# Side streams interleaved at smaller steps, and the decay's 64-row matmuls split over the two halves of the array

## The chip, the cores and the metric

One Trainium2 chip, one core of it. The metric is the time of one execution on the device in microseconds (us), as the median of several runs. TensorE is PE in the profile, VectorE DVE, ScalarE ACT, GpSimd POOL, and SyncE (SP) issues the DMAs.

## The reference

Two layers of a trunk with four gated branches run over 640 tokens: 128 context tokens and 512 latent tokens, of width 1024, in fp32. What a layer computes, cut to what matters here:

```python
h = rmsnorm(x, g_norm) * (1 + scale) + shift
(a_u, a_v, b_r, b_k, b_v, b_wd, b_ad, c_q, c_k, c_v, d_p, z, mg) = split_in(h @ w_in)
# RWKV-7 mixer, for both directions d
decay = exp(-exp(-softplus(-(w0[d] + tanh(b_wd) @ w_up[d])) - 0.5))
a = sigmoid(a0[d] + b_ad @ a_up[d])          # b_ad has ICL_RANK = 64 columns
k_d = k * (1 + (a - 1) * k_a)
S = S * w - (S kk) (kk * a)^T + v k_d^T       # scan over the tokens, o = S r
y_b = group_norm(o_sum) * ln_g + ln_b + bonus
# attention (windowed, with sinks), chunk mixer, pool mixer; then
ys = stack(y_a, y_b, y_c, y_d) * silu(z)
x = x + gate * ((sum over branches of sigmoid(mg) * (ys @ w_up)) @ w_o)
```

## The kernel before

Features lie on the 128 partitions and tokens on the free axis, in two halves `hs[0]` and `hs[1]` of HF = 320 tokens. The large products (`accum`, the **main stream**) take each operand as a high and a low part in fp32r (`hi`, `lo`, and for weights `whi`, `wlo`), three one-pass matmuls of 128x320 for a tile of 128 inputs: 7008 in all, in four `m` banks of PSUM. Weights come as `raw` pieces by DMA; `split` (L435) casts them to `whi` on ACT and subtracts for `wlo` on DVE.

All else is **side streams**: generators that `Clock.run` (L227) advances between steps of the main stream. The order of the whole program is set there, while it is built. `Clock` keeps estimates of when each operand is ready; a side stream that yields is resumed when its estimated time has come, and what stands between two of its yields is issued in one piece. Streams that matter here:

- `normed` (L620): the norm and modulation of x for the next layer, with `rstd_thin` (L599), which sums squares over the partitions by 128x2 matmuls (`x<-cst,nacc` for the sum `acc`, `x<-cst,t` for its last part `more`), takes the root (ACT) and the reciprocal `rst` (DVE), and spreads it over the partitions by transposing matmuls (`x<-cst,rst`, the function `spread`).
- `scan(ft, ...)` (L695), one for each half ft of the mixer's features, one after the other. Its `decay(d)` (L707) is called for both directions: two 64-row matmuls (`x<-adt,pb`, 64x320, fp32) give the learning rate a for the two halves of tokens, each read by three ACT instructions; then the decay `w` by `x<-pb,wdt`, by `x<-cst,A` and by ACT's Exp. Between the directions `vn` is reversed by matmuls with `anti` (`x<-vn,cst`). Then come the masked products (`x<-qr,kb`), 31 dependent steps on DVE that invert the blocks, eight rounds of the recurrence, and at the end `group_norm` (L983) is spawned as a stream of its own (`x<-yb,cst`, then the variance `x<-t,cst`).
- `attention` (L1164): its scores are pairs of 64-row matmuls (`x<-xm`), one head on the lower and one on the upper array rows, each into its own bank.

The side streams share two `x` banks (`X()`), the recurrence and the attention's values the banks `c` and `o`. `head` (L1315) makes `ck`, `cv`, `q0` and `q1`; in layer 0 the first three are accumulated together over all eight tiles of h as these become ready, and `put` then copies them out of PSUM, on ACT and DVE in turn. `adt` holds the mixer's b_ad on partitions 64 to 127, `aup` its weights on the same rows:

```python
px = X()
mm(px[:, 0:HF], ap[64:128, d, ft * P:(ft + 1) * P], adt[64:128, hs[b]])
A.activation(th[:, hs[b]], px[:, 0:HF], AF.Tanh, bias=a0h[:, 2 * d + ft:2 * d + ft + 1], scale=0.5)
```

Of the kernel before, what the change touches and what calls it, by code (L numbers as in the profile page):

```python
# [14 lines left out]
P = 128  # L15
# [44 lines left out]


DRAM = set()


def _box(ap):
# [230 lines left out]
def hybrid_layers_kernel(ctx: ExitStack, tc: tile.TileContext, xt, cond, condb, wm, wt, wa, wb, wo, pa, pb, pc, gfin, kctx, vctx,  # L296
# [302 lines left out]
    def rstd_thin(acc, more=None):  # L599

        ms = X()
        parts = [acc] if more is None else [acc, more]
        for i, o in enumerate((0, P, HF - P)):
            for x in parts:
                mm(ms[:, 2 * i:2 * i + 2], x[:, o:o + P], K("mean")[:, 0:2], start=i == 0 and x is acc,
                   stop=i == 2 and x is parts[-1])
        st = S([P, 6], "rst", 2)
        A.activation(st, ms[:, 0:6], AF.Sqrt, bias=eps[:, 0:1])
        V.reciprocal(st, st)

        def spread():
            bc = X()
            for i, (o, c) in enumerate(((0, 0), (P, 0), (2 * P, C))):
                mm(bc[:, o:min(o + P, HF)], st[:, 2 * i:2 * i + 1].to_broadcast([P, P]), K("ident")[:, c:P])
            A.copy(acc, bc[:, 0:HF])
            return bc

        return spread

    def normed(xs, accs, l, out, bs, ahead, more=None):  # L620
        rs = {}
        for b in bs:
            rs[b] = accs[b]
            if l:
                rstd_thin(accs[b], more)()
        for b in bs:
            out[b] = (S([P, KT, HF], f"hi{b}", dt=F32R), S([P, KT, HF], f"lo{b}", dt=F32R))
            ck.mark(f"hh{l}{b}")
# [42 lines left out]
    def layer(l, h, prb):  # L671
# [23 lines left out]
        def scan(ft, ta, kt, rt, vt):  # L695
# [9 lines left out]
            wup = prm("wup").rearrange("p (f d c) -> p f d c", f=2, d=2)  # L705

            def decay(d):  # L707
                for b in range(2):
                    px = X()
                    mm(px[:, 0:HF], ap[64:128, d, ft * P:(ft + 1) * P], adt[64:128, hs[b]])  # L710
                    A.activation(th[:, hs[b]], px[:, 0:HF], AF.Tanh, bias=a0h[:, 2 * d + ft:2 * d + ft + 1], scale=0.5)
                    A.activation(kd[:, hs[b]], th[:, hs[b]], AF.Identity, bias=kab[:, ft:ft + 1],
                                 scale=kah[:, ft:ft + 1])
                    A.activation(th[:, hs[b]], th[:, hs[b]], AF.Identity, bias=eps[:, 3:4], scale=0.5)
# [70 lines left out]
            for d in range(2):  # L785
# [15 lines left out]
                yield from keys(d)  # L801
                if d == 0:
                    yield from decay(1)
            yield
            for b in range(2):
                px = X()
# [95 lines left out]
            for j in range(8):  # L902
# [78 lines left out]
                state.update(nxt_state)  # L981
                yield
            def group_norm():  # L983
                oc = [X(), X()]
                cen = S([P, 2, HF], "v")
                sqs = []
# [328 lines left out]
        def head():  # L1315
# [17 lines left out]
            if l == 0:  # L1333
# [5 lines left out]
                for k in range(KT):  # L1339
                    turn = k % 4 == 3  # L1340
                    for b, i in [(b, i) for i in range(3) for b in range(2)] if turn else [
                            (b, i) for b in range(2) for i in range(3)]:
                        yield f"h{l}{b}.{k}"
                        yield from accum([out[i][b]], ws[i], k % 4, 1, [rhs_h[b]], k, k == 0, k == KT - 1)
                        if turn and b:
                            if k + 1 < KT:
                                ws[i] = piece(0)
                            else:
                                split(nxt[2] + i)
                yield f"n{l}0"  # L1350
                for i in range(3):
                    for b in range(2):
                        put(HEAD[i], b, out[i][b])
                o = yield from main()
                for b in range(2):
                    put(HEAD[3], b, o[b])
# [47 lines left out]
        o = yield from main()  # L1404
        for b in range(2):
            A.activation(wdt[0:64, hs[b]], o[b][0:64, :], AF.Tanh)
            V.tensor_copy(adt[64:128, hs[b]], o[b][64:128, :])
        ck.mark(f"{L}wa")
        for n, t in (("k0", ta[:, 0]), ("v0", vt), ("r0", ta[:, 2]), ("k1", kx[:, 0]), ("r1", kx[:, 1]), ("v1", kx[:, 2])):
            yield from main_to(t)  # L1410
# [189 lines left out]
def _layout(inputs):  # L1600
# [42 lines left out]
    wup[:, 0:64] = g["rw_w_up"].reshape(NL, 2, 64, 2, P).transpose(0, 2, 3, 1, 4).reshape(NL, 64, 512)  # L1643
    wup[:, 64] = g["rw_w0"].reshape(NL, 2, 2, P).transpose(0, 2, 1, 3).reshape(NL, 512)
    aup = np.zeros((NL, P, 512), np.float32)
    aup[:, 64:] = g["rw_a_up"].transpose(0, 2, 1, 3).reshape(NL, 64, 512)
    pw = np.zeros((NL, P, 2, P), np.float32)
    for gr in range(4):
        r = slice(64 * (gr % 2), 64 * (gr % 2) + 64)
# [38 lines left out]
```

## Time and profile before

| | us |
|---|---|
| median of 3 runs (lowest, highest) | 1394.77 (1393.83, 1397.92) |
| profiled execution, its own time | 1396.28 |
| span from its first to its last instruction | 1394.2 |
| PE busy in the span | 1349.6 (97%), 11350 instructions |
| DVE busy | 925.8 (66%), 2056 instructions |
| ACT busy | 565.3 (41%), 1258 instructions |
| POOL busy | 48.0 (3%), 43 instructions |
| mean granted clock of PE | 0.992 |

Busy times are unions of an engine's instructions. Matmuls overlap, so a matmul's own duration (0.31 us for a main one) is longer than the step to the next (0.147 us). An fp32 matmul shows as two instructions, a transpose or an fp32r matmul as one. The column of idle time counts from the modelled end of the last instruction. A granted clock of 1.00 is 2.4 GHz, of 0.50 it is 1.2 GHz.

### The profile page before, as it was taken

What the parts mean: (1) busy time and instruction counts of PE and PEld (TensorE: products, weight loads), DVE (VectorE), ACT (ScalarE), POOL (GpSimd) and SP (SyncE); (2) the same over time, 40 slices, a digit from 0 to 9 for tenths busy, and PEclk for the clock granted to TensorE, in tenths of its full rate; (3) what the DMA queues carried; (4) which work ended last, traced back from release to release, by engine and by line L of the source; (5) the groups of instructions that cost most, each with busy time, mean ns of one, the idle gap of its engine ahead of it and who ended that gap; (6) DMA issues with size and microseconds to landing.
All of it is one profiled execution on the core that took longest, in us unless ns stands there. A gap on an engine that the chain in (4) does not pass through costs nothing. (4 is left out here: it accounts for less than half of the span.)

```text
span 1394.2 us, 27698 instructions
## 1 busy us (share of the span) xinstructions
PE 1349.6 (97%) x11350; PEld 1259.7 (90%) x11350; DVE 925.8 (66%) x2056; ACT 565.3 (41%) x1258; POOL 48.0 (3%) x43
## 2 busy tenths in 40 slices
PE   5899999999999999999999999999999999999997
PEld 4889889988999988999999988898799998899997
DVE  5766677856777856658876667694377684464474
ACT  5455622234522333325555555223354233332364
POOL 0100010000000000000001001000000000000000
PEclk9999999999999999999999999999999999999998
DMA  9411133421224331751113212433022323144012
GB/s 376 148 54 61 39 108 106 108 81 66 67 88 115 106 94 63 267 187 61 61 62 120 72 54 66 109 87 88 24 60 65 89 83 82 37 157 156 22 39 76
DMA packets 86503, 132.61 MB, mean 95 GB/s; under 512 B 44744, under 2 KB 46152, under 8 KB 84456
## 3 DMA queue, kind: packets, MB, share of 16 engines
q1 hardware_dynamic: 86376, 130.84, 29.9%
q8 instruction: 89, 1.46, 0.4%
q14 instruction: 38, 0.31, 0.1%
HBM read 120.46 MB, written 10.35 MB: 94 GB/s over the span
## 5 line engine op out<-in xcount | busy, mean ns | idle before, releaser
L331 PE MATMUL m<-hi,whi 128*128 128x320 f32 x2064 | 666.1, 323 | 3.3 <-ACT whi L290 1.6
L331 PE MATMUL m<-hi,wlo 128*128 128x320 f32 x2064 | 641.4, 311 | 1.9 <-DVE wlo L290 1.9
L331 PE MATMUL m<-lo,whi 128*128 128x320 f32 x2064 | 640.6, 310 | 2.0 <-DVE lo L290 1.3
L331 PEld LDWEIGHTS m<-hi,whi 128*128 128x128 f32 x2064 | 389.9, 189 | 25.3 <-issue 10.2
L331 PEld LDWEIGHTS m<-lo,whi 128*128 128x128 f32 x2064 | 390.1, 189 | 5.1 <-DVE lo L290 2.0
L331 PEld LDWEIGHTS m<-hi,wlo 128*128 128x128 f32 x2064 | 389.5, 189 | 4.5 <-DVE wlo L290 4.2
L290 ACT CAST whi<-raw 128x640 fp32r<-128x640 f32 (+1 forms) x220 | 148.9, 682 | 282.3 <-PE m L331 262.6
L290 DVE TENSOR_TENSOR wlo<-raw,whi 128x640 fp32r<-128x640 f32 (+1 forms) x220 | 168.1, 769 | 107.6 <-ACT whi L290 104.8
L290 ACT ACTIVATE t<-m 128x320 f32<-128x320 f32 x152 | 64.2, 434 | 87.3 <-PE m L331 87.1
L290 DVE TENSOR_TENSOR kb<-kb 80x31 f32<-80x31 f32 (+15 forms) x248 | 86.2, 348 | 10.2 <-DMA kb<-ad 3.5
L290 DVE SCALAR_TENSOR_TENSOR t<-t,m 128x320 f32<-128x320 f32 x120 | 57.7, 481 | 47.0 <-PE m L331 38.0
L331 PE MATMUL m<-ysh,whi 128*128 128x320 f32 x256 | 82.6, 323 | 0.7 <-DVE t L290 0.7
L290 DVE CUSTOM_DVE_ANT_0 junk<-wt,sil 128x1024 bf16<-128x1024 f32 x64 | 79.2, 1237 | 3.8 <-DMA wt<-wt 3.6
L331 PE MATMUL m<-ysh,wlo 128*128 128x320 f32 x256 | 79.1, 309 | 0.0
L331 PE MATMUL m<-ysl,whi 128*128 128x320 f32 x256 | 79.0, 309 | 0.0
L290 DVE TENSOR_TENSOR xm<-xm,t 128x320 f32<-128x320 f32 x96 | 50.8, 530 | 3.3
L331 PEld LDWEIGHTS m<-ysh,whi 128*128 128x128 f32 x256 | 48.1, 188 | 3.4 <-DVE t L290 0.9
L331 PEld LDWEIGHTS m<-ysl,whi 128*128 128x128 f32 x256 | 48.2, 188 | 0.2
L331 PEld LDWEIGHTS m<-ysh,wlo 128*128 128x128 f32 x256 | 48.1, 188 | 0.0
L290 DVE RECIPROCAL t<-t 128x320 f32<-128x320 f32 x16 | 34.4, 2149 | 19.1 <-ACT t L290 19.1
L290 ACT ACTIVATE vn<-c 64x128 f32<-64x128 f32 x40 | 10.8, 271 | 79.0 <-DVE vn L290 79.0
L290 DVE TENSOR_TENSOR A<-x,cst 128x512 f32<-128x512 f32 x40 | 25.7, 684 | 20.6 <-PE x L331 20.6
(242 smaller groups left out, 1517.8 us busy)
## 6 DMA issues: line engine op xcount, KB each, us to landing
raw<-wb SPq DMA_DIRECT2D x128, 320.0 KB, 2.9
raw<-wa SPq DMA_DIRECT2D x92, 256.0 KB, 2.9
wt<-wt SPq DMA_DIRECT2D x32, 512.0 KB, 4.0
A<-wm SPq DMA_DIRECT2D x4, 1024.0 KB, 9.1
A<-wo SPq DMA_DIRECT2D x8, 512.0 KB, 6.0
xm<-xt SPq DMA_DIRECT2D x4, 640.0 KB
ad<-A SPq DMA_DIRECT2D x8, 320.0 KB
qr<-wm SPq DMA_DIRECT2D x2, 1024.0 KB
```

The lines of the kernel that those rows point to most:

```text
L290: return f(out, *a, **k)
L331: PE.matmul(out, lhsT, rhs, start=start, stop=stop)
```

## The change

The sums in `rstd_thin` go over `acc` first and then over `more`; `normed` yields between the sums and the spread; `decay` issues its two matmuls together, the first half of tokens on array rows 64 to 127 and the second on rows 0 to 63, for which `adt`'s second half and a second copy of `aup` lie on the lower partitions; `scan` yields once more behind the second direction's decay; `group_norm` yields before its first matmul; and `head` in layer 0 puts each tile as soon as its last product is issued.

```diff
+ROWS = (slice(64, 128), slice(0, 64))
...
         parts = [acc] if more is None else [acc, more]
-        for i, o in enumerate((0, P, HF - P)):
-            for x in parts:
+        for x in parts:
+            for i, o in enumerate((0, P, HF - P)):
                 mm(ms[:, 2 * i:2 * i + 2], x[:, o:o + P], K("mean")[:, 0:2], start=i == 0 and x is acc,
                    stop=i == 2 and x is parts[-1])
...
             if l:
-                rstd_thin(accs[b], more)()
+                spread = rstd_thin(accs[b], more)
+                yield
+                spread()
...
             def decay(d):
-                for b in range(2):
-                    px = X()
-                    mm(px[:, 0:HF], ap[64:128, d, ft * P:(ft + 1) * P], adt[64:128, hs[b]])
+                pxs = [X(), X()]
+                for b, px in enumerate(pxs):
+                    mm(px[:, 0:HF], ap[ROWS[b], d, ft * P:(ft + 1) * P], adt[ROWS[b], hs[b]])
+                for b, px in enumerate(pxs):
                     A.activation(th[:, hs[b]], px[:, 0:HF], AF.Tanh, bias=a0h[:, 2 * d + ft:2 * d + ft + 1], scale=0.5)
...
                 yield from keys(d)
                 if d == 0:
                     yield from decay(1)
+                    yield
...
             def group_norm():
+                yield
                 oc = [X(), X()]
...
                         yield from accum([out[i][b]], ws[i], k % 4, 1, [rhs_h[b]], k, k == 0, k == KT - 1)
+                        if k == KT - 1:
+                            yield f"n{l}0"
+                            put(HEAD[i], b, out[i][b])
...
-                yield f"n{l}0"
-                for i in range(3):
-                    for b in range(2):
-                        put(HEAD[i], b, out[i][b])
...
-            V.tensor_copy(adt[64:128, hs[b]], o[b][64:128, :])
+            V.tensor_copy(adt[ROWS[b], hs[b]], o[b][64:128, :])
...
-    aup[:, 64:] = g["rw_a_up"].transpose(0, 2, 1, 3).reshape(NL, 64, 512)
+    for r in ROWS:
+        aup[:, r] = g["rw_a_up"].transpose(0, 2, 1, 3).reshape(NL, 64, 512)
```

As the order comes from the estimates in `Clock`, nearly every piece of the side streams stands beside other main matmuls than before. The main matmuls keep their order; POOL's instructions keep theirs. Of the changes between a matmul of the main stream and one of a side stream there were 520 on PE and are 542; of changes of the array's size (tiles of 128, 64 or 32 rows or columns) between neighbours there were 416 and are 415.

PE in layer 1, at the end of the first scan: the decay of the second scan (`adt,pb`) and the group norm of the first (`yb,cst`). Before:

```order
L331 MATMUL m<-hi_7953,wlo 128x320
L331 MATMUL x<-adt,pb 128x320 x2
L331 MATMUL x<-yb,cst 128x320 x2
L331 MATMUL m<-hi_7571,whi 128x320
L331 MATMUL m<-lo_7572,whi 128x320
```

and now:

```order
L332 MATMUL m<-hi_7971,wlo 128x320
L332 MATMUL x<-adt,pb 128x320 x2
L332 MATMUL m<-hi_7580,whi 128x320
L332 MATMUL m<-lo_7581,whi 128x320
L332 MATMUL m<-hi_7580,wlo 128x320
```

The decay is followed by main matmuls, and `yb,cst` comes after 15 of them. Between `cst,A` and the reversal `vn,cst` no main matmul stood in any of the four scans; now 36, 12, 15 and 12 do.

PE in layer 1, the norm of the second half of tokens (`nacc` and `t` are summed, `rst` is spread). Before:

```order
L331 MATMUL m<-hi_7571,wlo 128x320
L331 MATMUL x<-cst,nacc 128x2
L331 MATMUL x<-cst,t 128x2
L331 MATMUL x<-cst,nacc 128x2
L331 MATMUL x<-cst,t 128x2
L331 MATMUL x<-cst,nacc 128x2
L331 MATMUL x<-cst,t 128x2
L331 MATMUL x<-cst,rst 128x128 x2
L331 MATMUL x<-cst,rst 128x64
L331 MATMUL m<-hi_7571,whi 128x320
```

and now:

```order
L332 MATMUL x<-cst,nacc 128x2 x3
L332 MATMUL x<-cst,t 128x2 x3
L332 MATMUL m<-hi_7580,whi 128x320
L332 MATMUL m<-lo_7581,whi 128x320
L332 MATMUL m<-hi_7580,wlo 128x320
L332 MATMUL m<-hi_7580,whi 128x320
L332 MATMUL m<-lo_7581,whi 128x320
L332 MATMUL m<-hi_7580,wlo 128x320
L332 MATMUL x<-cst,rst 128x128 x2
L332 MATMUL x<-cst,rst 128x64
```

Six main matmuls stand between the sums and the spread.

ACT in layer 0's head (`xm<-m` and `xm<-c` are the copies of ck and q0, `bon<-m` that of cv, `whi` the next weights, `wt<-sil` belongs to the modulation). Before:

```order
L290 ACTIVATE wt<-sil 128x1024
L290 CAST whi<-raw 128x512
L290 ACTIVATE wt<-sil 128x1024
L290 CAST whi<-raw 128x512 x2
L290 COPY xm_642<-m 128x320
L290 COPY bon<-m 128x320
L290 COPY xm_642<-c 128x320
```

and now:

```order
L291 ACTIVATE wt<-sil 128x1024
L291 COPY xm_606<-m 128x320
L291 CAST whi<-raw 128x512
L291 ACTIVATE wt<-sil 128x1024
L291 COPY bon<-m 128x320
L291 CAST whi<-raw 128x512
L291 COPY xm_606<-c 128x320
L291 CAST whi<-raw 128x512 x2
```

The copies stand between the casts. DVE, which makes the second copy of each tile, has them in the same way; there ck's copy and the rotation of ck that follows now come ahead of the low part of q1's second weights.

## Rows read from the trace of the kernel before

**Rows 1.** The page's first part: busy us, share of the span, instructions.
```profile
PE 1349.6 (97%) x11350; PEld 1259.7 (90%) x11350; DVE 925.8 (66%) x2056; ACT 565.3 (41%) x1258; POOL 48.0 (3%) x43
```
**Rows 2.** Waits of PE: who waited for whom, us in total, times, longest.
```profile
PE x L331 <- ACT A L290: 4.9, 6, 1.4
PE x L331 <- DVE rst L290: 2.5, 4, 0.7
```
**Rows 3.** Timeline of PE: start, us until the end, instruction, count; a decay.
```profile
375.98 1.34 PE L331 MATMUL x<-adt,pb 64*128 64x320 f32 x4
...
376.62 0.70 PE L331 MATMUL x<-adt,pb 64*128 64x320 f32 x2
...
376.89 0.43 PE L331 MATMUL x<-adt,pb 64*128 64x320 f32 x1
377.25 0.41 PE L331 MATMUL m<-hi,whi 128*128 128x320 f32 x1
```
**Rows 4.** Timeline of PE: a pair of the attention's scores.
```profile
149.12 0.70 PE L331 MATMUL x<-xm 64*128 64x256 f32 x4
149.75 0.41 PE L331 MATMUL m<-hi,whi 128*128 128x320 f32 x1
```
**Rows 5.** Timeline of PE, layer 0: the reversals of both scans [idle before, releaser].
```profile
168.84 1.41 PE L331 MATMUL x<-vn,cst 64*64 64x512 f32 x8 [1.39 <-ACT A L290]
170.18 0.44 PE L335 MATMUL o<-cst,kbt 128*128 128x128 f32 x2
...
385.15 1.08 PE L331 MATMUL x<-vn,cst 64*64 64x512 f32 x4
...
386.76 0.41 PE L331 MATMUL m<-hi,whi 128*128 128x320 f32 x1
```
**Rows 6.** Timeline of PE, layer 0: the first group norm.
```profile
331.62 0.81 PE L331 MATMUL x<-yb,cst 128*128 128x320 f32 x2
333.31 0.81 PE L331 MATMUL x<-yb,cst 128*128 128x320 f32 x2 [0.89 <-ACT A L290]
...
335.71 1.24 PE L331 MATMUL x<-t,cst 128*128 128x320 f32 x4
```
**Rows 7.** Timeline of PE, layer 1: the first group norm.
```profile
1006.35 1.32 PE L331 MATMUL x<-yb,cst 128*128 128x320 f32 x2 [0.89 <-ACT A L290]
...
1010.33 1.24 PE L331 MATMUL x<-t,cst 128*128 128x320 f32 x4
```
**Rows 8.** Stretches: length, busy of PE, PEld, DVE, ACT, POOL, clock, DMA.
```profile
1006.50:1009.90 3.40, 3.40 (x12) 3.01 (x13) 0.49 (x1) 3.02 (x5) 0.00 (x0) 0.50 0.00 0
...
712.90:716.30 3.40, 3.40 (x16) 3.40 (x15) 1.61 (x3) 1.50 (x4) 0.00 (x0) 0.51 0.78 267
```
**Rows 9.** Timeline of PE: the spread of the second half's norm, layer 1.
```profile
711.56 0.85 PE L331 MATMUL x<-cst,rst 128*128 128x128 f32 x6 [0.68 <-DVE rst L290]
```
**Rows 10.** Timeline of DVE: first and last of the eight rounds behind it.
```profile
715.16 1.00 DVE L290 SCALAR_TENSOR_TENSOR t<-xm,gsc,nacc 128x320 f32<-128x320 f32 x2
...
731.87 0.55 DVE L290 SCALAR_TENSOR_TENSOR lo<-t,shift,hi 128x320 fp32r<-128x320 f32 x1 [0.17 <-ACT hi L290]
```
**Rows 11.** Timeline of PE: layer 0's head, from q0's last matmuls on.
```profile
57.52 0.31 PE L331 MATMUL o<-hi,whi 128*128 128x320 f32 x1
...
57.81 0.31 PE L331 MATMUL o<-hi,wlo 128*128 128x320 f32 x1
59.57 0.41 PE L331 MATMUL m<-hi,whi 128*128 128x320 f32 x1 [1.44 <-ACT xm L290]
...
62.51 0.39 PE L331 MATMUL m<-hi,whi 128*128 128x320 f32 x1
```
**Rows 12.** Timeline of DVE: a product of the modulation, layer 0's head.
```profile
58.92 1.23 DVE L290 TENSOR_TENSOR sil<-wt,sil 128x1024 f32<-128x1024 f32 x1
```
**Rows 13.** Timeline of PE and of DVE, layer 1: the second group norm.
```profile
1213.28 1.24 PE L331 MATMUL x<-yb,cst 128*128 128x320 f32 x4
...
1224.06 0.55 DVE L290 SCALAR_TENSOR_TENSOR yb<-v,pb,bon 128x320 f32<-128x320 f32 x1
```

## The prediction

> **What bounds the kernel now.** I read the page first: the share of each engine says that TensorE (PE) is busy for 1349.6 of 1394.2 us [rows 1]. So a DMA, a cast or a vector operation is worth nothing here unless PE waits for it, and there are only two ways to gain: make PE's own work shorter, or take away places where it stands still. The second view is therefore the list of waits of PE alone; two lines of it belong to places that the change touches: matmuls into the x banks wait 4.9 us in all for ACT to read the bank, and 2.5 us for the reciprocal `rst` [rows 2]. The third is the timeline of PE at each place that the diff names, because the idle column understates a wait: a matmul's modelled end lies well behind its successor's start, so I count from start to start. The step of a main matmul (128x320, one pass) is 0.147 us there: 57.52 to 57.81 is two steps [rows 11]. The fourth is the order of the program before and after: it shows where each piece of the side streams now stands between the 7008 main matmuls, which themselves keep their order.
>
> **1. The decay's two matmuls on different array rows.** Eight calls, each with two 64-row matmuls of 320 columns, four instructions in the trace. On the same rows they run one after the other: from 375.98 to the next main matmul at 377.25, 1.27 us [rows 3]; the third and the fourth stand 0.27 apart, which is what one of them streams. The trace has the new form in the attention's scores, where the two heads stand on the lower and the upper rows and write two banks: four instructions of 256 columns need only 0.63 us from 149.12 to the next main matmul at 149.75 [rows 4]. One instruction of 256 columns streams 4/5 as long as one of 320, so four in line would be about 1.27 - 4 x 0.05 = 1.06 us: the pair saves two of four steps. For 320 columns that is 1.27 - 2 x 0.27 = 0.73, a gain of 0.54 a call and **-4.3 us** for eight. It lies on PE's own path, so nothing has to hide anything. The bounds are two steps (-4.3) and one (-2.2); I take two, as the scores have the same form to the letter.
>
> Here a rule of the Trainium skill speaks for less. TensorE: Matmul & The Clock Gate, Part 3, says that matmuls start and end strictly in the order of issue. If the two instructions of one matmul were issued ahead of the two of the other, only the middle ones could overlap, and this term would be -2.2. The scores' row disagrees: with one overlap their block would be about 1.06 - 0.21 = 0.85, not 0.63.
>
> **2. A yield behind the second decay.** The reversal of v (`anti`) took the x bank that the decay's Exp still read. In both layers' first scan PE is idle 1.39 us for ACT [rows 5]; once begun, the block takes 1.34 there, from 168.84 to 170.18. In the second scans it takes 1.61, from 385.15 to 386.76, so 0.27 more, for the same bank. In the new order at least 12 main matmuls (1.76 us) stand between `cst,A` and the reversal at all four places, more than the wait was. 2 x 1.39 + 2 x 0.27 = **-3.3**; what covers it is main work that PE has to do anyway.
>
> **3. A yield ahead of the group norm.** Its first matmuls followed the decay of the second scan with nothing between. The first norm matmul starts at 331.62 and the second at 333.31, 1.69 later [rows 6], where two instructions of 320 columns need 0.54. The difference is 1.15; as a block of its own the norm costs one more change of array size, about 0.1 (the decay's last instruction is followed after 0.36 instead of 0.27 [rows 3]). I take -1.05 in each layer, **-2.1**, bounds -0.9, the idle time shown, and -1.15. Fifteen main matmuls (2.2 us) now stand in the gap. In layer 1 the same stall has a second price. From the second norm matmul to the variance matmul there are 12 main matmuls in both layers: 2.40 us in layer 0 [rows 6], 3.98 in layer 1 [rows 7]. In that stretch the granted clock is 0.50, the level of 1.2 GHz [rows 8], and PE had just stood still. Without the stall I expect no such stretch: **-1.6**, bounds 0 and -1.6.
>
> **4. The norm of layer 1: all of acc first, and a yield ahead of the spread.** The 12 tiny matmuls cost the same in either order. The wait for the reciprocal is idle time of 0.68 in the second half's norm, at 711.56 [rows 9], and the first half's norm has one of the same kind; six main matmuls (0.88 us) now fill each. After the second one the clock also falls to 0.51 for 3.4 us [rows 8], which costs about 13 steps x 0.12 = 1.56. But what is late next here is the chain of DVE and ACT that makes h of the second half: eight rounds from 715.16 to the last lo at 731.87 [rows 10], about 2.1 us each, while PE gets through its 96 covered matmuls in 14 us and must then wait for h. In the new order the spread falls directly behind the last matmul of ck and should be through near 712.8; with ACT's copy of it and a multiplication that now stands first on DVE the chain starts near 713.9, some 1.2 earlier, an estimate. So of 0.7 + 1.56 only 1.2 comes through; for the first half, whose chain is as tight, I take 0.5. Together **-1.7**, bounds -0.5 and -3.9.
>
> **5. Earlier puts in layer 0's head.** q1's first matmul waits for a bank of ck: 57.81 to 59.57 instead of 0.147, thus 1.6, and the transposes of cv then wait about 1.0 more until 62.51 [rows 11]. With the copies behind each tile both go. But the copies and ck's rotation now stand in DVE's queue ahead of the low part of q1's second weights, with the second multiplication of sil before them (1.23 at 58.92 [rows 12], then a shuffle and two products). Adding these up, cv's second copy ends near 62.5 and the low part near 63.1, where PE would want the copy at 61.7. PE is through main matmul 168 and the transposes at about 63.3, where before it was at 64.8 (62.51 and 15 more main steps): **-1.5**, bounds 0 and -2.6. Of the DMAs, ck's output now stands on SP's queue ahead of two loads of raw weights; it waits for ck's second copy, near 57.4, and the loads are wanted some 5 us later: nothing, or +1 if they are late.
>
> **6. What is added.** The changes of array size between neighbours stay at 416 against 415, but 22 more changes between main and side matmuls come in, 11 more blocks. A change costs nothing where the array's size stays and about 0.1 where it doesn't [rows 3]: 0 to 2.2. Every side step now falls beside another main step, and the existing waits of 0.3 (ACT's negated vn ahead of kbt, the low parts on DVE) will be dealt anew; I add **+2.5** for both, bounds 0 and +6. POOL's order is the same and all 22 loads of ACT tables stay, so nothing for these. In layer 1 the second scan ends 48 main matmuls later; that is priced under the rivals.
>
> Sum: -4.3 - 3.3 - 2.1 - 1.6 - 1.7 - 1.5 + 2.5 = -12.0. The profiled execution takes 1396.28, so the change gives 1384.3; the median of the runs shown is 1.5 below the profiled one, and on that footing I forecast **1383.0 us**.
>
> **The rivals.**
> (a) The waits come back elsewhere: DVE and ACT have as much to do as before, and where they feed PE nearly without reserve (the heads) an earlier PE only waits later. For it: part 4's chain; against it: behind every decay and every group norm the new order has nothing but covered main work. Then the decay's 4.3, the clock's 1.6 and about 2 of the rest stay, less 2.5: -5.4, **1389**.
> (b) Both instructions of the decay's first matmul are issued ahead of the second's, so that only the middle two overlap: one step of 0.27 saved in a call instead of two. For it: the program issues them so; against it: the scores' row. -12.0 + 2.2 = -9.8, **1385**.
> (c) All waits vanish and nothing new comes: -14.5, and up to -3.3 more by the far bounds of parts 4 and 5: 1377 to 1380, **1379**.
> (d) Slower: the second scan of layer 1 becomes the bound. Its chain is serial, starts later by 42 to 48 main matmuls in the new order, and the last merge needs it. The group norm's last matmul now stands 126 main matmuls (18.5 us) ahead of the first DVE product that reads yb, and the chain from its first matmul at 1213.28 to yb takes about 11 us, to 1224.6 [rows 13]. So it has 7.5 us left and costs nothing. It decides once the scan slips by more than that beyond the order; a slip of 25 us would cost 17 and give **1400**. Nothing in the trace shows such a slip, as PE sets the pace there too.
>
> **How the numbers follow.** Forecast 0.60, (a) 0.20, (b) 0.10, (c) 0.06, (d) 0.04. About 0.3% (4.2 us) is what a measurement can tell from no change, so faster means below 1390.6: all of forecast, (b) and (c), and two thirds of (a), 0.89. A third of (a), 0.07, lies within it, and (d) is slower. For 8 in 10 the range reaches from 1378, in the middle of (c), to 1390, which holds most of (a).
>
> **What would show each step.** The four instructions of a decay followed by a main matmul after 0.73 instead of 1.27, or after 1.0 by (b). No idle time for ACT ahead of the reversal and the norm. A granted clock of 1.00 behind layer 1's first group norm and its second spread. A main matmul at once behind the last product of q0. The waits of PE for ACT (4.9) down to about 1, for `rst` down to what the end of the kernel has. Wrong would be: the same sum of waits under other names (a), long waits ahead of the last merge of layer 1 (d), or new stretches at half clock.

## The result, and the profile after

The changed kernel takes **1382.64 us** (median of 4 runs, 1381.10 to 1383.47) beside 1395.54 for the kernel before in the same session (4 runs): ratio 0.9904, 95% interval 0.9887 to 0.9920, so 12.9 us faster. The forecast was 1383.0 with the range 1378 to 1390. The experiments below show that this hit is worth less than it looks: the prices of the edited places held, but what the change as a whole brings hangs on something that the prediction had put down as a small constant. The two executions whose profiles are read below lie further apart than the medians: 1396.28 and 1381.10, thus 15.2.

The page's first part of the changed kernel (its span is 1379.3 us), against [rows 1]:

```profile
PE 1339.5 (97%) x11350; PEld 1253.4 (91%) x11350; DVE 926.0 (67%) x2056; ACT 565.7 (41%) x1258; POOL 51.8 (4%) x43
```

The busy time of TensorE (PE) fell by 10.1 us and the span by 14.9; the other engines do the same work. The waits of PE of the changed kernel (who waited for whom, us in total, times, longest), against [rows 2]:

```profile
PE m L332 <- DVE wlo L291: 2.8, 8, 1.0
PE x L336 <- DVE bon L291: 1.7, 1, 1.7
...
PE m L332 <- ACT t L291: 1.5, 3, 0.8
...
PE x L332 <- DVE rst L291: 1.3, 2, 0.7
```

The line of 4.9 us for ACT's `A` is gone, and `rst` has only its two waits at the end of the kernel. `bon`, `wlo` and ACT's `t` have grown in their place (0.8, 1.9 and 0.3 in the kernel before).

**Where the time went.** The 7008 main matmuls keep their order. So the start of main matmul n in one trace less its start in the other, freed of what the first one differs by (they start at 25.12 and 25.61 us here), tells how much was won up to n. In stretches of nothing but main matmuls this difference is constant, and one can subtract from one such plateau to the next:

| main matmuls | place | measured, us | terms of the prediction there |
|---|---|---|---|
| 96 to 192 | layer 0's head | -0.8 | -1.5 |
| 192 to 1056 | layer 0, first scan | -2.7 | 2 decays, reversal: -2.5 |
| 1056 to 2592 | layer 0, second scan, both group norms | -3.1 | 2 decays, reversal, norm: -2.4 |
| 3168 to 3744 | layer 1's norm | -1.6 | -1.7 |
| 3744 to 4608 | layer 1, first scan | -1.6 | -2.5 |
| 4608 to 6240 | layer 1, second scan, both group norms | -4.5 | 2 decays, reversal, norm, clock: -4.0 |
| 6816 to 6912 | the last norm | -1.5 | 0 |
| all | | -15.8 | -14.5 (before rounding), and +2.5 for added blocks and new waits |

**The decay.** Timeline of PE of the changed kernel (start, us until the end, instruction, count), two of the eight calls, against [rows 3]:

```profile
79.20 1.12 PE L332 MATMUL x<-adt,pb 64*128 64x320 f32 x4
80.25 0.42 PE L332 MATMUL m<-hi,whi 128*128 128x320 f32 x1
...
131.93 0.81 PE L332 MATMUL x<-adt,pb 64*128 64x320 f32 x4
132.67 0.41 PE L332 MATMUL m<-hi,whi 128*128 128x320 f32 x1
```

Seven calls take 0.74 instead of 1.27: two of the four instructions start within 0.01 us of each other, and the other two 0.37 later, again together. The first call takes 1.05, because its second x bank is still being read by DVE:

```profile
78.77 0.69 DVE L291 CUSTOM_DVE_ANT_0 kbt<-x,xm 128x512 f32<-128x512 f32 x1
```

Its four instructions start at 0, 0.32, 0.37 and 0.69 us, so the two of the late matmul stand 0.37 apart as well, 0.32 behind those of the other. A pair overlaps as far as both its banks are free.

**Reversals and group norm.** PE in layer 0, the reversals of both scans, against [rows 5], and layer 1's first group norm, against [rows 7]:

```profile
156.92 1.29 PE L332 MATMUL x<-vn,cst 64*64 64x512 f32 x8
158.15 0.44 PE L336 MATMUL o<-cst,kbt 128*128 128x128 f32 x2
...
385.48 1.29 PE L332 MATMUL x<-vn,cst 64*64 64x512 f32 x8
386.70 0.41 PE L332 MATMUL m<-ysh,whi 128*128 128x320 f32 x1
...
998.78 1.24 PE L332 MATMUL x<-yb,cst 128*128 128x320 f32 x4
999.62 0.55 PE L332 MATMUL m<-hi,whi 128*128 128x320 f32 x1
...
1002.98 0.41 PE L332 MATMUL m<-hi,whi 128*128 128x320 f32 x1 [0.76 <-ACT t L291]
```

No idle time stands ahead of either; a reversal takes 1.23 everywhere and the norm's first four instructions 0.84 instead of 2.1 in layer 0 and 2.35 in layer 1. But 3.4 us behind them a main matmul waits 0.76 for ACT, where the kernel before had nothing of the kind. The stretches behind this norm and behind the second spread of layer 1's norm now run at the full 2.4 GHz, against the 0.50 and 0.51 of [rows 8] (length, busy of PE, PEld, DVE, ACT, POOL, clock, DMA):

```profile
706.30:709.70 3.40, 3.40 (x27) 3.40 (x26) 2.96 (x6) 2.60 (x6) 0.00 (x0) 1.00 0.96 307
998.80:1002.20 3.40, 3.40 (x20) 2.83 (x19) 1.49 (x3) 2.17 (x6) 0.00 (x0) 1.00 0.02 5
```

**The head.** PE, DVE and POOL in layer 0's head, against [rows 11, 12]:

```profile
58.30 0.31 PE L332 MATMUL o<-hi,wlo 128*128 128x320 f32 x1
58.44 0.31 PE L332 MATMUL m<-hi,whi 128*128 128x320 f32 x1
...
61.97 0.38 PE L336 MATMUL x<-cst,bon 128*128 128x128 f32 x2
64.05 0.55 PE L336 MATMUL x<-cst,bon 128*128 128x128 f32 x3 [1.71 <-DVE bon L291]
64.35 0.39 PE L332 MATMUL m<-hi,whi 128*128 128x320 f32 x1
```

```profile
62.91 0.69 DVE L291 TENSOR_TENSOR xm<-xm,vn 128x512 f32<-128x512 f32 x1 [1.16 <-POOL xm L291]
63.51 0.48 DVE L291 COPY bon<-m 128x320 f32<-128x320 f32 x1
```

```profile
61.15 1.72 POOL L291 TENSOR_TENSOR xm<-xm,xm 128x512 f32<-128x512 f32 x1 [46.89 <-DVE vn L291]
```

The wait for q1's bank is gone (0.14 from q0's last product to q1's first). The transposes of cv wait longer than before, 1.71: cv's second copy ends at 63.99. That is a full us behind the forecast of 62.5, even less the 0.5 by which this whole execution began later: ck's rotation, ahead of it in DVE's queue, waits for a product on POOL that the prediction had left out.

### The profile page after: what moved, and what is told of

It is laid out like the page before. It is cut to its first block, busy times and chain, and to the rows that moved or that the text cites. A ratio compares the mean times of both kernels' runs of the same rounds, so it can differ in the third digit from the quotient of the medians.

```text
span 1379.3 us, 27713 instructions
## 1 busy us (share of the span) xinstructions
PE 1339.5 (97%) x11350; PEld 1253.4 (91%) x11350; DVE 926.0 (67%) x2056; ACT 565.7 (41%) x1258; POOL 51.8 (4%) x43
## 4 chain that ended last, share of the span: by engine, by line
PE 83%; issue 6%; DVE 5%; ACT 3%; DMA 1%; POOL 1%; SPq 0%; POOLq 0%; DVEq 0%; ACTq 0%
PE m L332 65%; PE x L332 9%; PE c L332 5%; PE o L332 2%; DVE wlo L291 2%; DVE t L291 1%; ACT whi L291 1%; PE x L336 1%; DMA qr<-wm 1%; PE o L336 1%; DMA xm<-xt 1%; PE c L336 0%; ACT vn L291 0%; DVE kb L291 0%; ACT hi L291 0%
## 5 line engine op out<-in xcount | busy, mean ns | idle before, releaser
L291 DVE TENSOR_TENSOR wlo<-raw,whi 128x640 fp32r<-128x640 f32 (+1 forms) x220 | 171.8, 784 | 106.2 <-ACT whi L291 102.4
L291 DVE CUSTOM_DVE_ANT_0 kbt<-x,xm 128x512 f32<-128x512 f32 (+3 forms) x56 | 26.8, 516 | 19.7 <-PE x L332 19.7
```

What stands on the lines that cost most here:

```text
L291: return f(out, *a, **k)
```

## The experiments

The theory on trial: the edits are independent, and their prices, read from the places they touch, add up. The main rival: the planner deals all later side blocks anew after every edit, and this deal weighs as much as the edits. (A side block is what stands of the side streams between two main matmuls; the deal is the list of the main matmuls that the blocks stand behind.) Each edit was taken alone and taken away alone, but for the yield behind the decay, which was only taken away. "Main matmul n" counts as above. Medians of the kernel before in these sessions: 1396.5, 1396.7, 1396.7 and 1397.0; the changed kernel again, below: 1382.1, to which the removals are compared, also those of other sessions.

| run | median, us | ratio to before, 95% interval | forecast from the edited places |
|---|---|---|---|
| pair alone | 1394.99 | 0.9993, 0.9982 to 1.0004 | 1391.2 |
| group norm's yield alone | 1401.21 | 1.0038, 1.0026 to 1.0051 | 1391.8 |
| norm alone | 1393.43 | 0.9973, 0.9961 to 0.9985 | 1393.8 |
| head alone | 1401.31 | 1.0035, 1.0023 to 1.0047 | 1395 |
| all but the pair | 1388.05 | 0.9943, 0.9928 to 0.9957 | 1387 |
| all but the head | 1388.33 | 0.9942, 0.9923 to 0.9960 | 1384 |
| all but the group norm's yield | 1396.99 | 1.0002, 0.9992 to 1.0012 | 1386.3 |
| all but the decay's yield | 1391.63 | 0.9962, 0.9950 to 0.9975 | 1386 |
| all but the norm | 1393.51 | 0.9971, 0.9958 to 0.9984 | 1384.4 |
| changed, ck's rotation later | 1395.07 | 0.9988, 0.9979 to 0.9997 | 1379 |
| changed again | 1382.07 | 0.9889, 0.9876 to 0.9903 | 1382 to 1384 |
| changed, one step nudged | 1390.91 | 0.9959, 0.9945 to 0.9973 | 1382 to 1383 |

### The pair alone, and all but the pair

```
+ROWS = (slice(64, 128), slice(0, 64))
...
-                for b in range(2):
-                    px = X()
-                    mm(px[:, 0:HF], ap[64:128, d, ft * P:(ft + 1) * P], adt[64:128, hs[b]])
+                pxs = [X(), X()]
+                for b, px in enumerate(pxs):
+                    mm(px[:, 0:HF], ap[ROWS[b], d, ft * P:(ft + 1) * P], adt[ROWS[b], hs[b]])
+                for b, px in enumerate(pxs):
...
```

The cut shows the edit as it was made alone; the lines that fill `adt` and `aup` belong to it. The removal undoes it, and so below.

> The kernel before with the decay's two matmuls on different rows and no other edit; all 2302 side matmuls stand between the same main matmuls as before. If the pair's gain lies on PE's own path: every one of the 8 decays is followed by its next matmul after about 0.73 us instead of 1.27 (the two at 330 and 1003 us after about 0.9 instead of 1.42), -4.3 us in all, 1391.2 beside a 1395.5. If only one step overlaps (b): 1.0 us a call, -2.2. If what PE saves is waited for elsewhere (a): 0.73 a call, but the stalls behind the second decays of both first scans (1.45 us for ACT ahead of the reversal) grow by as much, and the gain is -2 to -3.

> The changed kernel with the decay's two matmuls on the same rows again; its order on PE is the changed kernel's. If gains add up: 1.27 us a call and 4.3 slower than the changed kernel, about 1387 (8.6 faster than before). If the yields only moved waits about and the pair carries the change: within 2 us of the kernel before. If the pair's saving is hidden in the new order: within 1 us of the changed kernel.

Neither edit moves a single side matmul against the kernel it is compared with, so here the price is measured without a new deal. Alone it brings 1.5 us (interval +0.6 to -2.5), not 4.3. PE of the kernel with the pair alone, the first decay of layer 0's second scan and behind it the group norm, and a main matmul behind the next decay:

```profile
331.86 0.81 PE L332 MATMUL x<-adt,pb 64*128 64x320 f32 x4
333.28 0.81 PE L332 MATMUL x<-yb,cst 128*128 128x320 f32 x2 [0.61 <-ACT A L291]
334.97 1.21 PE L332 MATMUL x<-yb,cst 128*128 128x320 f32 x2 [0.89 <-ACT A L291]
...
384.00 0.42 PE L332 MATMUL m<-hi,whi 128*128 128x320 f32 x1 [0.47 <-ACT t L291]
```

The pair is done 0.68 earlier, and the norm behind it waits 0.61 longer for the same bank: 1.42 from the decay to the norm, as before. So two calls give nothing, in the second scans of both layers 0.47 is lost to ACT (at 384.00 and 1056.00), the first call gives 0.01 and one 0.42. What the second call gives goes in a wait for DVE: 0.97 at 239.76, where the kernel before waits 0.50. Rival (a) of the prediction is what happens here, though at other places than my expectation named.

In the order of the changed kernel the same edit is worth 6.0 (1388.05 against 1382.07). The decays' own part is 3.3, by the differences between the two traces: 0.24, 0.50, 0.52, 0.51, 0.42, 0.54 and 0.53, and nothing from the one at main 4866, whose 0.54 comes back in the wait at 1002.98 (idle 0.76 there, 0.22 with the pair taken out). The rest of the profiled difference (6.35 between the two traces) is two stretches at half clock, 1.5 each, behind stalls that both kernels have:

```profile
707.95:711.36 3.41, 3.41 (x16) 3.41 (x17) 2.59 (x5) 1.21 (x3) 0.00 (x0) 0.50 0.95 294
1346.24:1349.65 3.41, 3.41 (x15) 3.41 (x15) 1.33 (x1) 1.57 (x4) 2.72 (x3) 0.50 0.02 5
```

What follows: the overlap is worth what the scores' row promised, if the next user of the banks isn't right behind it and DVE and ACT keep up. Two of the eight calls need the group norm's yield for it; that the other yields made the room for the rest is not shown.

### The group norm's yield alone, and all but it

```
             def group_norm():
+                yield
```

> The kernel before with only the yield at the start of the group norm. If the stall between the two halves' norm matmuls is what the term is: both stalls for ACT (0.94 us each) go, the stretch at half clock at 1006.5 us goes with the second, -2.1 and -1.6, together -3.7, 1391.8. If the new deal of the side blocks costs what it gains: 0 to -1.5, with other stalls of the same sum. If the stretches at half clock come and go by themselves: the one at 1006.5 is no more bound to go than those at 713 and 1355 us.

> The changed kernel without the yield at the start of the group norm. The norm follows the decay again in both layers (main 1347 and 4851). If the terms of the prediction add: 2.1 + 1.6 slower, 1386.3. If the pair also needs this yield, as the kernel with the pair alone says (its two decays ahead of a norm kept 1.42): 2 x (1.05 + 0.68) = 3.5 and up to 1.5 for a stretch at half clock, 1386 to 1388. If the yield is a loss here too, as alone on the kernel before: faster than 1382.

Alone it makes the kernel 4.7 us **slower**; no expectation had that sign. Both stalls ahead of the second half's norm did go. But the side stream of layer 0 now runs later, and its last group norm falls on main matmul 2544, behind which no main work may go on until that norm is done. PE there:

```profile
557.62 1.33 PE L331 MATMUL x<-yb,cst 128*128 128x320 f32 x4
561.46 2.50 PE L331 MATMUL x<-t,cst 128*128 128x320 f32 x4 [2.51 <-ACT t L290]
563.29 0.94 PE L331 MATMUL m<-hi,whi 128*128 128x320 f32 x1
```

In the changed kernel six main matmuls stand between the same two:

```profile
543.23 1.24 PE L332 MATMUL x<-yb,cst 128*128 128x320 f32 x4
544.06 0.55 PE L332 MATMUL m<-ysh,whi 128*128 128x320 f32 x1
...
545.18 1.24 PE L332 MATMUL x<-t,cst 128*128 128x320 f32 x4
```

From main 2208 to 2688 the kernel with the yield alone loses 3.8 against the kernel before, 1.5 of it in a stretch at half clock. A second new stall, 2.41 for DVE at 918.42, with a stretch of its own, is in layer 1.

Taken out of the changed kernel the same yield costs 14.9 us, far more than I expected. The waits at the norms come back as they should (3.0 us in four waits for ACT's `A`). Three stretches at half clock (at 730, 891 and 1355, the second of 6.8 us) are another part. A third is layer 1's attention, which ends on main matmul 4320, another place that main work may not pass, with six side pieces in a row. PE there, without the first and the last of the six:

```profile
886.31 1.35 PE L332 MATMUL x<-qr,kb 64*128 64x128 f32 x16 [1.61 <-DVE y L291]
888.25 0.81 PE L332 MATMUL x<-t,pb 128*128 128x320 f32 x2 [0.59 <-DVE A L291]
888.89 0.61 PE L336 MATMUL x<-cst,kb 128*128 128x128 f32 x4
891.58 1.40 PE L332 MATMUL x<-t,pb 128*128 128x320 f32 x2 [2.07 <-DVE t L291]
```

The kernel before and the changed kernel have the last four of these pieces on main 4320 too, with a single wait. PE of the changed kernel:

```profile
882.69 0.70 PE L332 MATMUL x<-t,pb 128*128 128x320 f32 x2
...
885.07 0.81 PE L332 MATMUL x<-t,pb 128*128 128x320 f32 x2 [1.24 <-DVE t L291]
```

The edit isn't in the attention, nor in anything that the attention needs.

### All but the head, and the head alone

```
+                        if k == KT - 1:
+                            yield f"n{l}0"
+                            put(HEAD[i], b, out[i][b])
...
-                yield f"n{l}0"
-                for i in range(3):
-                    for b in range(2):
-                        put(HEAD[i], b, out[i][b])
```

> The changed kernel with the puts of layer 0's head back behind all three products. If the terms add: 1.5 slower than the changed kernel, 1384. If the yields need the room that the earlier head gives: layer 0's second scan starts 63 main matmuls later (its decay at main 1662 instead of 1599), its last group norm falls on main 2544 for all its matmuls, as in the kernel with the group norm's yield alone, so nothing stands between them: a stall of about 2.6 us for ACT ahead of the variance, some 1.2 more around it, thus 1.5 + 3.8 = 5.3 slower, about 1388.

> The kernel before with only the earlier puts of layer 0's head. By the prediction's term: -1.5, 1395 beside 1396.6. If what the removal of this edit showed (5.7) is the room it gives the side stream of layer 0: here nothing needs that room (the last group norm stands at main 2457 without it), so -1.0 at the head, and the new deal in layer 1, whose attention ends at main 4278 to 4296 instead of 4320, takes the stalls at 871 and 895 (1.03 and 1.29): about -3, 1393.5.

The removal costs 6.3, as the theory of the room said (5.3): layer 0's last group norm falls on main 2544 again, and from main 2208 to 2688 4.6 us are lost. Here PE waits little at the norm itself (0.51) and more for the weights behind it (2.06 for DVE's `wlo` at 567.78, then a stretch at half clock): the trace fits that what stands on that mark delays DVE too. So the earlier head is worth less by what it wins at the head, 0.5 in this order, than by the start of layer 0's side stream some 60 main matmuls earlier, which the yields then use up.

Alone the head makes the kernel 4.6 slower, where I had expected 1.5 to 3 faster. The head itself brings the same 0.8, and layer 0 behind it gains too. But between main 3168 and 4416, in layer 1's norm, attention and first scan, 5.9 us are lost, most visibly on PE here, where a stretch at half clock begins as well:

```profile
857.48 0.44 PE L335 MATMUL o<-cst,kbt 128*128 128x128 f32 x2
860.60 1.31 PE L331 MATMUL x<-bon,cst 128*128 128x320 f32 x2 [2.68 <-DVE bon L290]
```

### All but the decay's yield

```
                 if d == 0:
                     yield from decay(1)
-                    yield
```

> The changed kernel without the yield behind the second decay. If the term stands: the reversal waits for ACT in the first scans again (1.45 us each, and 0.2 to 0.3 more in the second scans), 3.3 slower, 1386. If the new deal of the side blocks pays for it: within 1 us of the changed kernel, since the first scan's reversal moves 36 main matmuls forward and everything behind it too.

9.6 slower instead of 3.3, and hardly by the wait that I had named: in the first scans the reversal is idle for ACT 0.17 (layer 0) and 0.61 (layer 1), where the kernel before has 1.39 in each. What stands in its place on PE, in layer 0's second scan and in layer 1:

```profile
383.46 2.41 PE L332 MATMUL x<-cst,A 128*128 128x128 f32 x10 [2.17 <-DVE A L291]
...
910.47 0.87 PE L332 MATMUL x<-t,pb 128*128 128x320 f32 x1 [3.79 <-DVE t L291]
```

Both stalls have stretches at half clock, 3.4 and 6.8 us long.

### The norm alone, and all but the norm

```
-        for i, o in enumerate((0, P, HF - P)):
-            for x in parts:
+        for x in parts:
+            for i, o in enumerate((0, P, HF - P)):
...
-                rstd_thin(accs[b], more)()
+                spread = rstd_thin(accs[b], more)
+                yield
+                spread()
```

> The kernel before with only the layer norm's edit (all of acc first, a yield ahead of the spread). By the prediction: the waits for rst at 678.7 and 711.6 us (0.7 and 0.8) go, the stretch at half clock at 713 goes too, but the chain of DVE and ACT behind it gives part back, -1.7, 1393.8. If the chain is no limit: -3 or more. If the chain is the whole limit: 0, with waits for whi, lo and wlo between 718 and 735 us as large as what went.

> The changed kernel with the layer norm as before. If the term stands: the two waits for rst are back (0.7 and 0.8), those of the chain behind them shrink by some of it, 1.7 slower, 1384.4; a stretch at half clock behind one of them adds up to 1.5. If the chain of DVE and ACT is the whole limit: within 1 us of the changed kernel.

Alone it brings 3.1 us (interval 2.1 to 5.4), more than the 1.7. From main 3168 to 3744 it behaves as in the changed kernel: both waits for `rst` go, and a new one comes, 0.95 for `wlo` at 711.80 (0.96 at 703.01 in the changed kernel). The profile of it has no stretch at half clock between the start and the end of the kernel, which may be why it gains more.

Taken out it costs 11.4, not 1.7. The waits for `rst` are back, and on PE the chain behind them is worse than in either kernel:

```profile
725.35 0.41 PE L332 MATMUL m<-hi,whi 128*128 128x320 f32 x1 [1.15 <-ACT whi L291]
...
730.71 0.41 PE L332 MATMUL m<-hi,whi 128*128 128x320 f32 x1 [1.15 <-ACT whi L291]
```

Behind it the attention of layer 1 ends in six pieces on main 4320, as without the group norm's yield (waits of 1.93, 0.59 and 1.23), and four stretches at half clock come in that the changed kernel has not, at 676, 710, 1055 and 1352; by an estimate of 1.5 each they make 6 of the 12.0 between the two traces.

### A stall aimed at: ck's rotation later

```
             dma(k_o[l], kr[:, 0:TP])
-            rotate(kr, 0)
             yield f"{L}cv"
...
+            rotate(kr, 0)
             yield f"{L}q0"
             rotate(q2[0], 1)
```

> The changed kernel with ck's rotation (a shuffle, two products and a sum on DVE and POOL) issued behind the transposes of cv instead of ahead of them. In the changed kernel cv's second copy on DVE comes at 63.5, behind the rotation's last sum, which waits for POOL until 62.9; the transposes then wait 1.76 us. If that queue is the reason, this wait goes to below 0.5 (-1.3), and main matmul 168 begins about 1.3 earlier. In layer 1 the attention's last four blocks no longer stand on main 4320 but at 4284 to 4296, so the waits there (0.9 and 1.3 us at 861 and 885) go too: -3.5 in all, 1379. If the new deal spoils another place: the first stall is gone, but the time stays at 1382 or above, with a stall of over 1 us that the changed kernel has not.

The aimed-at stall is gone. PE in layer 0's head, and in layer 1:

```profile
64.11 0.71 PE L336 MATMUL x<-cst,bon 128*128 128x128 f32 x5
64.57 0.39 PE L332 MATMUL m<-hi,whi 128*128 128x320 f32 x1
...
861.92 0.81 PE L332 MATMUL x<-bon,cst 128*128 128x320 f32 x2 [1.80 <-DVE bon L291]
```

That wins 1.95 us up to main 192, and shows that the rotation in DVE's queue was the reason. It doesn't tell DVE's own work on the rotation from its wait for POOL, as both left that place together. The kernel is 13.0 slower all the same: other stalls, such as 1.80 at 861.92, took its place in both layers, none of them near the edit.

### The changed kernel again

> The changed kernel once more, for more runs of it and a second profile. The stalls in the order of the program should be the same to 0.1 us in both profiles, but for the loads before the first main matmul. If the stretches at half clock follow from the stalls alone, they stand where the first profile has them (one at 27.6 us and the end); if they come by chance behind stalls, others appear, each for about 1.5 us, behind one of the stalls of 0.7 us or more (64, 703, 885, 1003, 1340 us). Median 1382 to 1384.

1382.07, and a second profile whose main matmuls, from the sixteenth on, agree with the first's to 0.05 us once the first one's start (27.27 and 25.61) is taken off. So for one order the stalls are the same each time. Nor did a stretch at half clock appear between the start and the end.

### The same instructions, dealt otherwise

```
-                yield
+                yield 0.5
                 yield from keys(d)
```

> The changed kernel with the same instructions and waits and the same 542 switches between main and side matmuls, but the planner holds the step behind the reversal back by 0.5 us in both scans; 1341 of the 2302 side matmuls then stand between other main matmuls. If only the edited places count, nothing is gained or lost: 1382 to 1383. If the deal of the side blocks weighs as much as the edits: several us slower; the one place that its order lets foresee is layer 0's last group norm, now on main 2544 for all its matmuls as in two kernels before, +3.8, thus 1386, more where stalls and stretches at half clock come on top.

The yield stands in a loop over both directions, so the step behind the plain transposes of v is held back as well. This settles the main question: not one instruction is added, removed or made longer, and the kernel is 8.8 us slower (1390.91). It is the only nudge that was tried. PE at layer 0's last group norm, and 50 main matmuls later:

```profile
554.54 1.33 PE L332 MATMUL x<-yb,cst 128*128 128x320 f32 x4
557.24 1.34 PE L332 MATMUL x<-t,cst 128*128 128x320 f32 x4 [1.37 <-ACT t L291]
...
567.82 0.42 PE L332 MATMUL m<-hi,wlo 128*128 128x320 f32 x1 [1.90 <-DVE wlo L291]
```

From main 2208 to 2688 it loses 3.85, the 3.8 that its order had let me foresee; about 2 more are lost in layer 1's norm and the chain behind it. It has no stretch at half clock at all before its end, so this is the deal alone.

## Why the prediction was right

The time was right (1383.0 forecast, 1382.64 measured), and the sign, and the forecast case was the one that came. That it was met so closely is luck in part. The sum was made for the profiled execution, and there 15.2 came instead of 12.0: the +2.5 wasn't seen, the head brought 0.7 less than forecast, and two stretches at half clock of the kernel before (at 1006 and 1355, 1.5 to 1.6 each), of which the sum held one, were not there again. Step by step:

**1. The decay: right.** 0.73 a call forecast, 0.74 in seven of eight; -4.3 forecast, 4.2 less between start and next matmul. Rival (b) is out: all seven calls with free banks took 0.74, none 1.0. The rule of the Trainium skill that spoke for it (TensorE: Matmul & The Clock Gate, Part 3) would have made the term -2.2; the measurement decides against that reading of it and for the scores' row. Where one bank was late, the four instructions start at 0, 0.32, 0.37 and 0.69 in the changed kernel and at 0, 0.37, 0.52 and 0.90 with the pair alone: the second instruction of one matmul starts behind the first of the other in one case and ahead of it in the other, so no fixed order of the four fits both. Two things were missed: the first call's bank, and 0.54 that a new wait at 1002.98 takes back. So 3.3 of the 4.3 is left in the changed kernel, and the sentence that this term "lies on PE's own path, so nothing has to hide anything" was wrong: alone, in the old order, most of it was waited for elsewhere.

**2. The yield behind the decay: right in the place, -3.8 for -3.3.** The blocks came out at 1.23 everywhere, shorter than the 1.34 I had left standing.

**3. The group norm: right.** The stalls and the stretch behind layer 1's norm went: the traces have -1.1 a layer and the 1.6. That the stall was bound to bring the stretch is not shown: with the pair alone the same stall of 0.89 stands there, and no stretch behind it. That the yield could by itself push the side stream over a mark and cost 4.7 was not seen.

**4. The norm of layer 1: right, -1.6 for -1.7**, and so was the reason for not counting the clock's 1.56 there. The pair alone happens to show it: it has the order of the kernel before, but no stretch at half clock behind the second spread, wins 1.5 by that at main 3552, and has given 1.3 back to waits for `whi` and `wlo` by main 3648.

**5. The head: mis-sized, -0.8 for -1.5.** The step that failed is the sum for DVE's queue, "cv's second copy ends near 62.5": it counted DVE's own work and not that the rotation's last sum waits there for POOL until 62.9, 1.16 of idle time on DVE. The run with the rotation later wins 1.95 there, more than the 0.7 missed, as it takes DVE's own work on the rotation away as well.

**6. What is added: this term was wrong in kind.** I gave "every side step now falls beside another main step" +2.5, between 0 and +6. As the table stands, next to nothing of it was seen: the rows sum to -14.3 without the last norm, where the terms without +2.5 sum to -14.5, and the last norm gave 1.5 that nobody had foreseen, a stretch at half clock that the profile of before has at 1354.66 and the two of after have not. That 1.5 is luck of the profiles: the wait ahead of it is in both kernels (below). But the same step is worth +8.8 in the nudged kernel, and the removals of the five edits cost 6.0, 6.3, 14.9, 9.6 and 11.4, together 48 us for a change of 14.6 in those sessions. Some of that is the clock: the profiles of the five removals hold 14 lengths of 3.4 us at half clock that the changed kernel's have not, at most 21 us by an estimate of 1.5 each; the nudged kernel's holds none. So the terms do not add up in general; they did for this one combination, whose deal is a good one. Nothing that I had argued told the deal that came from the others, and eight of the nine kernels above whose side blocks were dealt anew lie beyond 1390, the slow end of my range. It should have reached further on that side.

**Rival (d)** had the mechanism: a side stream that slips past the point where main work needs it. I looked for it only in layer 1's second scan; it decides in layer 0's last group norm (main 2544; 78 main matmuls behind its variance matmuls in the kernel before, 57 in the changed one) and, by the blocks on main 4320, in layer 1's attention. The first could be read from the order alone before any run, as in the nudged kernel (3.8 forecast, 3.85 lost there) and in the one without the earlier head (5.3 and 6.3 in all); of the second only the place: the kernel with the rotation later, whose order keeps these blocks off main 4320, was forecast to win 2.2 by that and loses 1.3 from main 3744 to 4608. What cannot be read from it are the many stalls of 0.3 to 2 us that a deal brings where DVE or ACT is late; what makes one deal have fewer of them than another was not settled.

No kernel tried here beats the changed one.

## What to carry to other kernels

Where a planner or a scheduler deals work into the gaps of a bound engine, price an edit twice: at its own place, and by where every block behind it lands; list the points that the main stream cannot pass, and count how far ahead of them each side stream ends before and after. Before believing in a gain, time one kernel with the same instructions and a small nudge to the order: if that moves the time as much as the edit, the edit's own worth has not been measured yet. A pair of half-height matmuls on different rows costs little more than one (0.74 here; one alone would be about 0.73, an estimate: 1.27 less two steps of 0.27), as long as both output banks are free and the next user of those banks is not right behind.

## What the runs showed of the hardware

Two 64-row matmuls of 320 float32 columns on different rows start within 0.01 us of each other and need 0.74 with the change back to full height, against 1.27 on the same rows. With the second bank late by 0.11, 0.32 and 0.52 us the four instructions need 0.85, 1.05 and 1.26.

The granted clock falls behind some waits of PE and not behind others, and no run here shows what decides. Stretches at half clock (1.2 GHz) of 3.4 us, sometimes two in a row, each cost 1.5 to 1.6 us, as pairs of profiles with the same order show. Each of the 22 between the start and the end of these 14 profiles begins within a wait of PE, or at most 2.2 us behind the end of one, of 0.58 us or more by the column of idle time; but there are some 170 such waits in them. The same wait in the same main work is followed by a stretch in one profile and not in another: all 14 profiles have 0.58 for `rst` at the last norm, on main 6828, and five of them a stretch behind it. PE in the kernel before, which has one, and in the changed kernel, which has none:

```profile
1353.45 0.88 PE L331 MATMUL x<-cst,rst 128*128 128x128 f32 x6 [0.58 <-DVE rst L290]
...
1339.69 0.88 PE L332 MATMUL x<-cst,rst 128*128 128x128 f32 x6 [0.58 <-DVE rst L291]
```

The Trainium skill says in TensorE: Matmul & The Clock Gate, Part 1, of the slow matmuls at a kernel's start that their number varies from run to run; these profiles show the like for stretches in the middle. So the 1.6 of step 3 is the price of a stretch that a stall may bring, and a stall less is worth a part of it on average.
